# Attention in a three-mixer encoder on one core: which operand of the value product is moved, and where the rows are divided by their sums

## The chip, the cores and the metric

The kernel runs on one core of a Trainium2 chip. The metric is device time in microseconds (us). The engines that matter here are PE (TensorE: matmuls, and weight loads called PEld), DVE (VectorE), ACT (ScalarE) and POOL (GpSimd); each works through its own queue in order, and semaphores hold an instruction until what it reads is there.

## What is computed

The reference is an encoder of two layers on 512 tokens of width 1024. Each layer has three token mixers (latent attention, an mLSTM, a state-space scan called SSD), an output projection, a layer norm and 16 experts. The change touches only the end of the attention:

```python
s = (einsum('bqhd,bkhd->bhqk', qn_b, k_nope) + einsum('bqhr,bkr->bhqk', qr_b, k_rope)) * scale
p = softmax(s, axis=-1)
o = einsum('bhqk,bkhd->bqhd', p, v)      # 8 heads, v is 64 wide, 512 queries, 512 keys
```

The softmax divides each row (a query) by the sum of its exponentials. Since that sum belongs to the query and not to the key, the division may come before the product with `v` or behind it.

## The kernel before, in words

Tokens lie in four tiles of 128 (`NT = 4`). The output projection wants the attention's result with features on the partitions and tokens along the free axis: `xh[j]` and `xl[j]`, the high and low parts of 128 features (two heads, pair `j`) by 512 tokens, which `finish_heads` (line 910) writes from PSUM with one ACT copy and one DVE subtraction.

`attention()` (line 1291) gives two generators.

- `scores(hd)`, five steps for a head. The first step makes the head's queries and keys. Each of the other four takes one tile of 128 queries: three matmuls (`mm3`) into a PSUM bank of 128 queries by 512 keys, a DVE reduction for the row's maximum, an ACT exponential that writes `P` (128x512, fp32) and the row's sum, a DVE reciprocal of that sum (128x1), and then the product of `P` with it in line 1339: on POOL for heads 0 to 5, on DVE for heads 6 and 7 (`NORMV`).
- `values(hd)`, four steps for a head and two more for every second head. Each of the four takes a block `c` of 128 keys: four PE transposes turn the four `P` blocks into `PT` (keys by 512 queries), which ACT or DVE copies to SBUF. Behind the odd head comes the product for the pair. For each key block and each of the two heads, `v` is the stationary operand (128 keys by 64 features) and `PT` is moved (128 keys by 512 queries):

```python
T.matmul(po_[64 * e:64 * e + 64], vt[c][:, (2 * j + e) * 64:(2 * j + e) * 64 + 64],
         PTs[2 * j + e][c].ap, start=(c == 0), stop=(c == NT - 1), skip_group_check=True)
finish_heads(j, po_.ap)
```

The first head of the pair fills partitions 0 to 63 of the bank and the second 64 to 127, so that the bank already has the form that `finish_heads` wants. All these operands are plain fp32. A plain fp32 product stands in the trace as two MATMUL records, each with a weight load of its own (the form printed is f32 for these and for the fp32r ones alike).

`SEQ` (line 72) is a hand-written string of the order in which steps of the mixers are written: d and h the SSD, p the projections, i the attention's inputs, m the mLSTM, s `scores`, v `values`. So attention and mLSTM alternate in one stretch of each layer (about 172 to 280 us and 680 to 788 us of the profile). Within it the framework that builds the program may still move instructions of different steps past each other on an engine's queue. PSUM has eight banks; three of them (`PA`, line 251) serve the attention's keys (`pk`), queries (`pq`) and `po_`, two (`PM`) the mLSTM, three (`PT_`) the scores and the transposes. SBUF slots come from one pool of 37, and from the same pool come the buffers into which the weights of the output projection and the experts are loaded ahead.

Behind the mixers comes the output projection (line 1622 on), which takes the feature blocks in the order 6 and 7, 4 and 5, 0 and 1, and at last 2 and 3 (`order = (3, 2, 0, 1)`).

Of the kernel before, what the change touches and what calls it, by code (L numbers as in the profile page):

```python
# [13 lines left out]
AF = mybir.ActivationFunctionType  # L14
OP = mybir.AluOpType
# [5 lines left out]
NT = S // 128  # L21
# [22 lines left out]
BLK = 96  # L44
POOLP = ()
AHEAD = 1
NORMV = (6, 7)
ZP = (2, 3)
PH = 512
RK = (0, 4)  # L50
# [135 lines left out]
class Buf:  # L186
# [4 lines left out]
    def free(self):  # L191
        assert self.live
        self.live = False
        self.pool.put(self)
# [17 lines left out]
def tile_trunk(ctx: ExitStack, tc: tile.TileContext, ins, out, dbg=None, depth=DEPTH):  # L212
# [3 lines left out]
    sm = ctx.enter_context(tc.tile_pool(name="sm", bufs=2))  # L216
# [18 lines left out]
    V, A, G, T = Pinned(nc.vector, "V"), Pinned(nc.scalar, "A"), nc.gpsimd, Pinned(nc.tensor, "T")  # L235
# [3 lines left out]
    def nm(s):  # L239
        cnt[0] += 1  # L240
        return f"{s}{cnt[0]}"
# [7 lines left out]
    Q, R = View(pool, F32R), View(pool, F32)  # L249
    banks = [psp.tile([128, 512], F32, name=f"b{i}") for i in range(8)]  # L250
    PA, PB = Slots(banks[0:NPA], 512), Slots(banks[NPA:8], 512)
# [4 lines left out]
    def small(shape, dt=F32, tag="s", bufs=1):  # L256
        return sm.tile(shape, dt, name=nm(tag), tag=tag, bufs=bufs)
# [97 lines left out]
    ident = const.tile([128, 128], F32, name="ident")  # L355
# [51 lines left out]
    def split(dst_h, dst_l, src, eng=V):  # L407
        r = A.activation(dst_h, src, AF.Copy)
        eng.tensor_sub(dst_l, src, dst_h.bitcast(F32))
        return r  # L410

    def pair(src=None):

        b = Q.get()
        h, lo = b.ap[:, 0:512], b.ap[:, 512:1024]
        if src is not None:
            split(h, lo, src)
        return b, h, lo

    def mm3(p, ah, al, bh, bl, start=True, stop=True):  # L420
        T.matmul(p, ah, bh, start=start, stop=False)
        T.matmul(p, ah, bl, start=False, stop=False)
        T.matmul(p, al, bh, start=False, stop=stop)
# [134 lines left out]
    for l in range(depth):  # L558
# [351 lines left out]
        def finish_heads(j, src, scale=None):  # L910
            h, lo = xh[j], xl[j]
            if scale is None:
                split(h, lo, src)
            else:
                A.activation(h, src, AF.Identity, scale=scale)
                V.scalar_tensor_tensor(lo, src, scale, h.bitcast(F32), op0=OP.mult, op1=OP.subtract)
# [366 lines left out]
        def load_uq(g):  # L1283

            r = R.get(1024)
            load(r.ap, ins["w_uqp"], (l * 2 + g) * 128 * 1024, [[1024, 128], [1, 1024]])
            res = [pair(r[:, k * 512:(k + 1) * 512]) for k in range(2)]
            r.free()
            return res

        def attention():
            rots = mla["rots"]
            qn, kn, (ukb, ukh, ukl), vt = (mla[n] for n in ("qn", "kn", "uk", "vt"))
            uqs, Ps, PTs, pks = {}, {}, {}, {}

            def scores(hd):
                j, e = hd // 2, hd % 2
                if hd % 4 == 0:
                    uqs[hd // 4] = load_uq(hd // 4)
                uq = uqs[hd // 4]  # L1300
                if e == 0:
                    pk = pks[j] = PA.get()
                    s = slice(j * 128, (j + 1) * 128)
                    T.matmul(pk.ap, ukh[:, s], kn[1], start=True, stop=False)
                    T.matmul(pk.ap, ukh[:, s], kn[2], start=False, stop=False)
                    T.matmul(pk.ap, ukl[:, s], kn[1], start=False, stop=True)
                pk = pks[j]
                pq = PA.get()
                for k in range(2):
                    h, lo = (t[:, (hd % 4) * 128:(hd % 4 + 1) * 128] for t in uq[k][1:])  # L1310
                    T.matmul(pq.ap, h, qn[k][1], start=(k == 0), stop=False)
                    T.matmul(pq.ap, h, qn[k][2], start=False, stop=False)
                    T.matmul(pq.ap, lo, qn[k][1], start=False, stop=(k == 1))
                qf = R.get_half()
                V.tensor_mul(qf.ap, pq.ap, rots.ap)
                pq.free()
                qb, qh, ql = pair(qf.ap)
                qf.free()
                _, kh, kl = kb[e]
                A.activation(kh[0:64], pk[64 * e:64 * e + 64], AF.Copy)  # L1320
                V.tensor_sub(kl[0:64], pk[64 * e:64 * e + 64], kh[0:64].bitcast(F32))
                if e:
                    pk.free()
                if hd % 4 == 3:
                    free([b for b, _, _ in uq])
                yield
                Ps[hd] = []
                for i in range(NT):
                    s = slice(i * 128, (i + 1) * 128)
                    pS = PT_.get()  # L1330
                    mm3(pS.ap, qh[:, s], ql[:, s], kh, kl)
                    mx = small([128, 1], tag="mx", bufs=6)
                    V.tensor_reduce(mx, pS.ap, axis=AX.X, op=OP.max, negate=True)
                    P = R.get_half()
                    sums = small([128, 1], tag="sums", bufs=6)
                    A.activation(P.ap, pS.ap, AF.Exp, bias=mx, accum_out=sums)
                    pS.free()
                    V.reciprocal(sums, sums)
                    (V if hd in NORMV else G).tensor_scalar(P.ap, P.ap, sums, 0.0, op0=OP.mult, op1=OP.add)  # L1339
                    Ps[hd].append(P)  # L1340
                    if i == NT - 1:
                        qb.free()
                    yield

            def values(hd):
                j, e = hd // 2, hd % 2
                PT = PTs[hd] = []
                for c in range(NT):
                    pb = PT_.get()
                    for i in range(NT):  # L1350
                        T.transpose(pb[:, i * 128:(i + 1) * 128], Ps[hd][i][:, c * 128:(c + 1) * 128], ident)
                    t = R.get_half()
                    if hd in PTV and c % 4 == 3:
                        V.tensor_copy(t.ap, pb.ap)
                    else:
                        A.activation(t.ap, pb.ap, AF.Copy)
                    pb.free()
                    PT.append(t)
                    if c == NT - 1:
                        free(Ps[hd])  # L1360
                    yield
                if e == 0:
                    return
                po_ = PA.get()
                for c in range(NT):
                    for e in range(2):
                        T.matmul(po_[64 * e:64 * e + 64], vt[c][:, (2 * j + e) * 64:(2 * j + e) * 64 + 64],
                                 PTs[2 * j + e][c].ap, start=(c == 0), stop=(c == NT - 1), skip_group_check=True)
                    if c == 1:
                        yield  # L1370
                free(PTs[2 * j], PTs[2 * j + 1])
                finish_heads(j, po_.ap)
                po_.free()
                yield

            return chain(scores), chain(values)

        def chain(f):
            for hd in range(HEADS):
                yield from f(hd)  # L1380
# [14 lines left out]
        for n, t in enumerate(SEQ):  # L1395
            ph({"m": "mlstm", "d": "ssd", "p": "proj"}.get(t, "attn"))
            if t == "s" and "s" not in streams:
                streams["s"], streams["v"] = attention()
            next(streams[t], 1)
# [417 lines left out]
        for c in WSEQ.split():  # L1817
            if c[0] == "Z":
                i = int(c[1])
# [36 lines left out]
        for _ in range(NU):  # L1856
            m, n = todo.pop(0)
# [295 lines left out]
        for i in range(NT):  # L2153
            n = norms[i]
# [79 lines left out]
```

## Time and profile before

| what | value |
|---|---|
| median of 3 runs | 1034.4 us (1031.29 to 1034.73) |
| profiled execution's own time | 1031.19 us |
| its span, first to last instruction | 1029.5 us |
| mean granted TensorE clock | 0.989 |
| HBM read, written | 159.61 MB, 23.59 MB |

The span lies within the profiled execution's own time; 1.7 us of that lie outside it. In a row that groups instructions, the first number after the bar is the time in which at least one of the group was running, the second the mean duration of one in ns; then comes idle time of the engine ahead of them and what ended it. Matmuls overlap, so the mean of one is longer than the pace at which they follow each other. In a windows row each engine has its busy time and its count of instructions in the stretch. In a waits row stand the total, the number of waits and the longest.

### The profile page before, as it was taken

What the parts mean: (1) busy time and instruction counts of PE and PEld (TensorE: products, weight loads), DVE (VectorE), ACT (ScalarE), POOL (GpSimd) and SP (SyncE); (2) the same over time, 40 slices, a digit from 0 to 9 for tenths busy, and PEclk for the clock granted to TensorE, in tenths of its full rate; (3) what the DMA queues carried; (4) which work ended last, traced back from release to release, by engine and by line L of the source; (5) the groups of instructions that cost most, each with busy time, mean ns of one, the idle gap of its engine ahead of it and who ended that gap; (6) DMA issues with size and microseconds to landing.
All of it is one profiled execution on the core that took longest, in us unless ns stands there. A gap on an engine that the chain in (4) does not pass through costs nothing. (4 is left out here: it accounts for less than half of the span.)

```text
span 1029.5 us, 15384 instructions
## 1 busy us (share of the span) xinstructions
PE 977.3 (95%) x5326; PEld 730.0 (71%) x5326; DVE 813.6 (79%) x1808; ACT 635.4 (62%) x1176; POOL 193.0 (19%) x176
## 2 busy tenths in 40 slices
PE   6999999999998899999999999999999989999995
PEld 6976697666687666766598767875657876667663
DVE  8996566878649799999969956578795498999986
ACT  5565635566424588889645555465673246888885
POOL 1000002242003143332100000022320122333422
PEclk9999999999999899999999999999999989999998
DMA  8201200115845889999542111001349387999943
GB/s 317 72 22 63 69 3 1 42 46 181 296 174 219 274 285 340 345 329 310 170 164 72 42 42 51 1 1 41 130 161 317 130 286 260 325 339 327 323 139 161
DMA packets 51795, 176.76 MB, mean 172 GB/s; under 512 B 8170, under 2 KB 8682, under 8 KB 51713
## 3 DMA queue, kind: packets, MB, share of 16 engines
q1 hardware_dynamic: 45216, 160.42, 43.9%
q0 software_dynamic: 6496, 15.31, 6.2%
q8 instruction: 43, 0.70, 0.3%
q14 instruction: 40, 0.32, 0.1%
HBM read 159.61 MB, written 23.59 MB: 178 GB/s over the span
## 5 line engine op out<-in xcount | busy, mean ns | idle before, releaser
L229 PE MATMUL b<-xt,s 128*128 128x512 f32 (+3 forms) x1488 | 326.1, 366 | 12.7 <-ACT s L229 9.2
L229 PE MATMUL b<-s,s 128*128 128x512 f32 (+8 forms) x1308 | 321.8, 404 | 4.7 <-ACT s L229 2.9
L229 PEld LDWEIGHTS b<-xt,s 128*128 128x128 f32 (+2 forms) x1488 | 233.1, 183 | 79.5 <-issue 12.2
L229 DVE TENSOR_TENSOR s<-s,s 128x1024 fp32r<-128x1024 f32 (+8 forms) x252 | 226.3, 922 | 53.4 <-ACT s L229 46.6
L229 ACT ACTIVATE s<-s 128x1024 fp32r<-128x1024 f32 (+4 forms) x220 | 191.3, 904 | 90.5 <-PE b L229 32.4
L229 PEld LDWEIGHTS b<-s,s 128*128 128x128 f32 (+3 forms) x1308 | 182.8, 171 | 85.2 <-ACT s L229 18.6
L229 ACT ACTIVATE s<-b 128x512 f32<-128x512 f32 (+8 forms) x274 | 131.8, 499 | 174.6 <-PE b L229 169.2
L229 PE MATMUL b<-s,xt 128*128 128x256 f32 (+2 forms) x944 | 203.5, 355 | 0.4 <-DVE s L229 0.3
L229 PEld LDWEIGHTS b<-s,xt 128*128 128x128 f32 (+1 forms) x944 | 146.3, 184 | 34.7 <-issue 6.7
L229 DVE TENSOR_TENSOR xt<-s,xt 128x1024 fp32r<-128x1024 f32 (+1 forms) x107 | 127.1, 1193 | 14.0 <-ACT xt L229 13.8
L229 ACT ACTIVATE xt<-s 128x1024 fp32r<-128x1024 f32 (+1 forms) x108 | 111.6, 1043 | 26.5 <-PE b L229 18.4
L229 PE MATMUL b<-ident,s 128*128 128x128 f32 (+3 forms) x736 | 106.2, 268 | 12.3 <-DMA s<-x1d,slx 5.5
L229 PEld LDWEIGHTS b<-ident,s 128*128 128x128 f32 (+3 forms) x736 | 80.7, 150 | 44.3 <-POOL s L1339 10.4
L1599 POOL DMA_INDIRECT acc<-s,slx x28 | 58.6, 2093 | 164.1 <-ACT s L229 121.0
L229 DVE TENSOR_TENSOR s<-b,s 128x192 fp32r<-128x192 f32 (+3 forms) x108 | 57.9, 549 | 12.7 <-PE b L229 10.1
L1339 POOL TENSOR_SCALAR s<-s,sums 128x512 f32<-128x512 f32 x48 | 37.3, 780 | 150.8 <-DVE sums L229 124.9
L229 ACT ACTIVATE s<-b,mx 128x512 f32<-128x512 f32 x64 | 43.9, 692 | 18.9 <-DVE mx L229 12.6
L1447 POOL DMA_INDIRECT s<-x1d,slx x30 | 40.9, 1365 | 56.2 <-PE b L229 21.4
L229 DVE TENSOR_REDUCE mx<-b 128x1 f32<-128x512 f32 x64 | 43.5, 686 | 8.9 <-PE b L229 8.0
L229 PE MATMUL b<-xt 128*96 128x512 f32 x160 | 47.6, 404 | 1.4 <-DVE xt L229 1.4
L229 ACT ACTIVATE s<-b,slw 96x512 f32<-96x512 f32 (+1 forms) x60 | 39.1, 683 | 5.6 <-PE b L229 3.6
L229 ACT ACTIVATE s<-s,sb 128x128 f32<-128x128 f32 x64 | 25.5, 412 | 19.2 <-DVE s L229 18.8
(249 smaller groups left out, 860.8 us busy)
## 6 DMA issues: line engine op xcount, KB each, us to landing
s<-in_w_gu_dram SPq DMA_DIRECT2D x128, 512.0 KB
s<-in_expert_w_down_dram SPq DMA_DIRECT2D x64, 512.0 KB
s<-in_w_inp_dram SPq DMA_DIRECT2D x36, 512.0 KB
s<-in_w_outp_dram SPq DMA_DIRECT2D x16, 512.0 KB
x1d<-s SPq DMA_DIRECT2D x8, 512.0 KB
acc<-s SPq DMA_DIRECT2D x8, 512.0 KB
s<-acc SPq DMA_DIRECT2D x8, 512.0 KB
s<-in_x_t_dram SPq DMA_DIRECT2D x4, 512.0 KB
```

The costliest lines, as they stand in the source:

```text
L229: r = f(*a, **kw)
L1339: (V if hd in NORMV else G).tensor_scalar(P.ap, P.ap, sums, 0.0, op0=OP.mult, op1=OP.add)
L1447: self.ga = G.indirect_dma_start(out=self.xg[:BLK], out_offset=None, in_=x1d[0:128 * n, :], in_offset=bass.IndirectOffsetOnAxis(ap=ix[:BLK ...
L1599: G.indirect_dma_start(out=acc[:, :], out_offset=bass.IndirectOffsetOnAxis(ap=self.ix[:BLK, 0:1], axis=0), in_=yt[:BLK], in_offset=None, b ...
```

## The change

The row sums of a pair of heads go into one tile of 128x4x2, and the reciprocal and the product in `scores` are gone, with `NORMV`: `P` holds plain exponentials. In the value product the operands change places: each 128x128 block of `PT` is the stationary operand and the 128x64 block of `v` is moved, so that the bank holds tokens on its partitions and, along the free axis, four token tiles of two heads of 64 features. One DVE reciprocal inverts the 128x8 sums, one DVE product reads the bank and writes it, scaled, to SBUF, four PE transposes turn that into a second bank of the same three, and `finish_heads` reads it from there.

```diff
-NORMV = (6, 7)
...
+                if e == 0:
+                    sums[j] = small([128, NT, 2], tag="sums", bufs=3)
...
-                    sums = small([128, 1], tag="sums", bufs=6)
-                    A.activation(P.ap, pS.ap, AF.Exp, bias=mx, accum_out=sums)
+                    A.activation(P.ap, pS.ap, AF.Exp, bias=mx, accum_out=sums[j][:, i, e:e + 1])
                     pS.free()
-                    V.reciprocal(sums, sums)
-                    (V if hd in NORMV else G).tensor_scalar(P.ap, P.ap, sums, 0.0, op0=OP.mult, op1=OP.add)
...
                 po_ = PA.get()
                 for c in range(NT):
                     for e in range(2):
-                        T.matmul(po_[64 * e:64 * e + 64], vt[c][:, (2 * j + e) * 64:(2 * j + e) * 64 + 64],
-                                 PTs[2 * j + e][c].ap, start=(c == 0), stop=(c == NT - 1), skip_group_check=True)
+                        for i in range(NT):
+                            o = (2 * i + e) * 64
+                            T.matmul(po_[:, o:o + 64], PTs[2 * j + e][c][:, i * 128:(i + 1) * 128],
+                                     vt[c][:, (2 * j + e) * 64:(2 * j + e) * 64 + 64], start=(c == 0 and i == 0 and e == 0),
+                                     stop=(c == NT - 1), skip_group_check=True)
                     if c == 1:
                         yield
                 free(PTs[2 * j], PTs[2 * j + 1])
-                finish_heads(j, po_.ap)
+                sm = sums[j].rearrange("p i e -> p (i e)")
+                V.reciprocal(sm, sm)
+                o = R.get_half()
+                V.tensor_tensor(o.v("p (n c) -> p n c", n=2 * NT), po_.v("p (n c) -> p n c", n=2 * NT),
+                                sm[:, :, None].to_broadcast([128, 2 * NT, 64]), op=OP.mult)
                 po_.free()
+                pt_ = PA.get()
+                for i in range(NT):
+                    T.transpose(pt_[:, i * 128:(i + 1) * 128], o[:, i * 128:(i + 1) * 128], ident)
+                o.free()
+                finish_heads(j, pt_.ap)
+                pt_.free()
                 yield
```

More of the change, by code (lines that the diff above doesn't have):

```diff
@@ L1293, in attention @@
             qn, kn, (ukb, ukh, ukl), vt = (mla[n] for n in ("qn", "kn", "uk", "vt"))
-            uqs, Ps, PTs, pks = {}, {}, {}, {}
+            uqs, Ps, PTs, pks, sums = {}, {}, {}, {}, {}
             def scores(hd):
```

## The prediction

> **What bounds the kernel now.** I read the page's busy times first, then the windows of the two stretches in which the attention runs, then the waits inside them. The chain of waits on the page is no help: its shares add up to 3% of the span, the last stage alone.
>
> ```profile
> span 1029.5 us, 15384 instructions
> PE 977.3 (95%) x5326; PEld 730.0 (71%) x5326; DVE 813.6 (79%) x1808; ACT 635.4 (62%) x1176; POOL 193.0 (19%) x176
> ...
> PE 1%; DVE 1%; ACT 1%; issue 0%; DVEq 0%; ACTq 0%
> ```
>
> PE is busy nearly throughout. The windows say whether that holds where the change is made; the third and fourth are the output projection that follows in the first layer.
>
> ```profile
> 172.00:280.00 108.00, 103.06 (x532) 69.35 (x532) 82.23 (x204) 67.60 (x156) 28.76 (x35) 1.00 0.37 127
> 680.00:788.00 108.00, 104.75 (x538) 70.03 (x538) 84.12 (x207) 68.49 (x157) 29.26 (x35) 1.00 0.38 126
> ```
>
> ```profile
> 282.00:292.00 10.00, 10.00 (x58) 8.51 (x57) 6.03 (x11) 1.08 (x2) 0.00 (x0) 1.00 0.89 305
> 292.00:302.00 10.00, 9.97 (x54) 8.26 (x54) 1.72 (x4) 2.15 (x3) 0.00 (x0) 1.00 0.14 37
> ```
>
> The columns after the length are PE, PEld, DVE, ACT and POOL. In the two stretches PE is idle for 4.9 and 3.3 us of 108, together 8.2 us; no other engine comes near it (DVE 82 and 84, ACT 68, POOL 29). So what the attention adds to PE's queue is paid nearly in full, and what it takes from DVE and POOL pays only through PE's few waits. PE's waits in the first stretch, then in the second:
>
> ```profile
> PE b L229 <- POOL s L1339: 1.6, 4, 0.6
> PE b L229 <- ACT s L229: 1.5, 4, 0.7
> PE b L229 <- DVE s L229: 1.3, 2, 0.9
> ```
>
> ```profile
> PE b L229 <- ACT s L229: 1.6, 4, 0.7
> PE b L229 <- POOL s L1339: 1.1, 3, 0.5
> ```
>
> Line 1339 is the product on the probabilities. Transposes that wait for it hold PE for 1.6 + 1.1 = 2.7 us in the whole kernel.
>
> **The value product.** Per pair of heads it is 4 key blocks by 2 heads, 8 products before and 8 by 4 token tiles, 32, behind the change; with 4 pairs and 2 layers 64 against 256. Each is two records on PE, so 128 against 512. The old ones are the only matmuls with 64 stationary and 512 moved columns in these stretches:
>
> ```profile
> L229 PE MATMUL b<-s,s 128*64 128x512 f32 x62 | 19.3, 610 | 0.7 <-ACT s L229 0.7
> ```
>
> ```profile
> L229 PE MATMUL b<-s 128*64 128x512 f32 x4 | 2.1, 605 | 0.0
> ```
>
> The first row stands in both stretches with the same numbers; the second is that of the whole kernel, for records whose two operands print alike. 62 + 62 + 4 = 128, the count wanted, and they took 19.3 + 19.3 + 2.1 = 40.7 us, 0.318 each. The mean of one is 0.610, so they overlap: the two heads of a pair fill different halves of the columns and in part run side by side.
>
> The new products, 128 stationary and 64 moved columns in plain fp32, do not stand in the trace, but a near twin does. The mLSTM multiplies a 128x128 fp32 block by 65 moved columns, 64 products in 128 records:
>
> ```profile
> L229 PE MATMUL b<-s,s 128*128 128x65 f32 x128 | 15.7, 271 | 0.0
> ```
>
> ```profile
> 227.83 2.39 PE L229 MATMUL b<-s,s 128*128 128x130 f32 x20
> ```
>
> By the first row a record costs 15.7 / 128 = 0.123 us. The second is a line of the timeline with 20 such records without a gap (the first few 130 wide, most 65): less the 0.271 of the last, 19 starts in 2.12 us, 0.112 each. That 130 and 65 columns follow at the same pace says that the moved columns do not set it; the weight load does, which every record has:
>
> ```profile
> L229 PEld LDWEIGHTS b<-s,s 128*128 128x128 f32 x656 | 100.6, 190 | 32.4 <-ACT s L229 15.1 <-DVE s L229 3.0 <-issue 2.0
> ```
>
> 656 of them in 100.6 us are 0.153 each, with gaps and other forms in it; I take that as a witness that loads of this size come no denser than about a tenth of a microsecond, not as a price. Between 0.112 and 0.123 I take 0.112, since the new products come in runs of 16 products whose operands lie ready: 512 x 0.112 = 57.3 us; with 0.123 it is 63.0. So the product alone costs 57.3 - 40.7 = 16.6 us more (22.3 with the other end).
>
> A rule of the Trainium skill speaks against this change in words: TensorEngine Tiling (Array Packing), in When to Use Tiling, says that where the moved side has at most 64 columns one should swap the operands and use two column tiles, for a gain of up to two. The kernel before is that swapped form. By the full factor the products would go to 81.4 us, 40.7 more; the rows above show only part of it, since the overlap before is partial.
>
> **The transposes.** Four for each pair, 32 in all, of 128x128 fp32, like those of the probabilities.
>
> ```profile
> L229 PE MATMUL b<-ident,s 128*128 128x128 f32 x416 | 69.7, 281 | 4.9 <-POOL s L1339 2.8 <-DVE s L229 1.0 <-ACT s L229 0.5
> ```
>
> ```profile
> 208.40 1.20 PE L229 MATMUL b<-ident,s 128*128 128x128 f32 x9 [0.21 <-POOL s L1339]
> ```
>
> 69.7 / 416 = 0.168 each with their tails; in the run of nine, (1.20 - 0.28) / 8 = 0.115. 32 of them are 3.7 to 5.4 us; I take 3.7, as they come in fours.
>
> **DVE, POOL and ACT.** What goes and what the new operations are like:
>
> ```profile
> L1339 POOL TENSOR_SCALAR s<-s,sums 128x512 f32<-128x512 f32 x48 | 37.3, 780 | 150.8 <-DVE sums L229 124.9
> ```
>
> ```profile
> L229 DVE TENSOR_TENSOR s<-b,s 128x512 f32<-128x512 f32 x32 | 21.6, 684 | 10.8 <-PE b L229 10.1 <-POOL s L1132 0.5
> ...
> L229 DVE RECIPROCAL sums<-sums 128x1 f32<-128x1 f32 x64 | 9.7, 155 | 3.6 <-ACT s L229 3.2
> ...
> L229 DVE TENSOR_SCALAR s<-s,sums 128x512 f32<-128x512 f32 x16 | 8.8, 558 | 0.1
> ...
> L229 DVE RECIPROCAL dn<-dn 128x8 f32<-128x8 f32 x8 | 1.5, 193 | 0.0
> ```
>
> POOL loses 37.3 us, all beside other work. DVE loses 9.7 + 8.8 = 18.5 and gains 8 x (0.193 + 0.684) = 7.0, so it gets 11.5 us lighter. PE waits on DVE for 1.3 us in the first stretch and not in the second; I count 1 us of it as gone. ACT keeps its exponentials, the readings of their sums and the copies. The 2.7 us that PE waited for line 1339 go; what is late next is the exponential itself, on ACT, from which these transposes then hang. ACT has room (68 of 108), but the earlier product also gave the queue time, so I count all 2.7 only because PE has more other work to do meanwhile.
>
> **The new wait.** In each pair the four transposes wait for the DVE product, that one for the last of the 32 matmuls, and behind the transposes PE's queue holds the next scores, mLSTM products and transposes. `finish_heads` waits in turn, one reciprocal, one product and four transposes later than before. If the framework puts them right behind the products, PE stands for 0.193 (if the reciprocal comes late), 0.684, and the rest of whatever DVE is doing; if other matmuls stand between, nothing. No such wait is in the trace of before, so I bound it by 0 and by two DVE operations of 0.684 and the reciprocal, 1.6 us, eight times: 0 to 12.5 us. The nearest row is PE's wait on DVE, 2 times and 1.3 us among all the DVE results that matmuls read in the first stretch, so I take a value near zero: 2 us in all. At the end of the stretch the wait has cover: the last pair is features 2 and 3 or earlier, the output projection takes these last, and the windows to 302 us show PE full. Should the cover be gone, it costs 1.6 us in each layer. The second bank comes from the same three (`PA`), with one more turn in each pair; a bank late by a DVE product is within the same bound.
>
> **The sum.** 16.6 + 3.7 - 2.7 - 1 + 2 = 18.6 us, against 1031.2 of the profiled execution: 1049.8. The median of the runs stands 3.2 us above that execution (1034.4), so the median should be 1053. Smallest: the low prices, all 8.2 us of PE's idle time gone, no new wait: 16.6 + 3.7 - 8.2 = 12.1, which is 1043.3 in the profile and 1046.5 as a median. Largest without the full new wait: 22.3 + 5.4 - 2.7 = 25.0, 1056.2 or 1059.4.
>
> **The rivals.**
>
> One: the moved columns set the pace after all, and the kernel gets faster. The old record costs 0.318 us for 512 columns, so one for 64 would cost 0.040, and 512 of them 20.4 us: 40.7 - 20.4 = 20.3 us less, with 3.7 for the transposes and 3.7 of waits gone, 1031.2 - 20.3 = 1010.9. It decides from the point where weight loads hide fully behind other matmuls, below 0.079 us a record (40.7 / 512). The skill's page TensorE: Matmul & The Clock Gate, Back-to-back issue gap, would even put 64 columns at about 60 cycles, 25 ns, which would make 12.8 us of the 512. Against it stand the 65-wide records at 0.112 and above, of the same kind and in the same queue. 3%.
>
> Two: PE is less full than it looks, since the ends of matmuls are modelled and a matmul that follows late looks joined. Then the added 20.3 us fill hidden gaps and the time stays within 3 us, 1028 to 1034 in the profile. For it: 10.4 us of weight loads waited on line 1339, of which only 2.7 show as PE idle.
>
> ```profile
> PEld b L229 <- POOL s L1339: 10.4, 18, 1.0
> ```
>
> Against it: all of that is 10.4, half of what is added, and the other waits of the loads, on ACT, stay. 4%.
>
> Three: the new wait is met in full, 12.5 us instead of 2: 1060.3 in the profile, 1063.5 as a median. For it: the transposes stand right behind the products in the program. Against: the framework already lets other steps' matmuls stand between a head's steps. It decides where fewer than about six scores matmuls are ready in the queue behind the products. 13%.
>
> Four: DMA sets the pace of the experts, and a later attention is made up there. The window to 302 us has a DMA share of 0.14: the loads ahead have run out of slots, so they start again only when the stages behind move, and everything moves with them. I give it no chance of its own.
>
> **How the numbers follow.** The forecast has 80%, rival one 3%, two 4%, three 13%. A measurement of this kernel tells from no change about 0.3%, 3 us. Faster 0.03, same 0.03 (most of rival two), slower 0.94. The range runs from 1043, the smallest sum with half of the spread of the runs (1.6 us, and 2 for what the order on PE's queue may bring), to 1064, rival three as a median.
>
> **What would show it.** In the profile of the changed kernel: 512 records of form 128*128 128x64 at 0.110 to 0.125 us each, 55 to 63 us; none of 128*64 128x512 in these stretches; 32 more transposes; no line 1339 on POOL; both stretches about 9 us longer, PE over 95% busy in them, the rest of the kernel as long as before. It would be wrong if the records came at under 0.09 or over 0.15 us, if PE's waits on DVE rose by over 5 us, or if the stretches grew by under 5 us each.

## The result and the profile after

| | before | changed |
|---|---|---|
| median of 4 runs each, us | 1034.57 (1031.29 to 1035.49) | 1048.88 (1043.56 to 1057.44) |
| profiled execution, us | 1031.19 | 1047.73 |

The ratio is 1.0138, with a 95% interval of 1.0101 to 1.0176: 14.3 us slower by the medians, where 18.6 were forecast.

The page of the changed kernel answers to the two lines quoted first in the prediction:

```profile
span 1046.0 us, 16076 instructions
PE 994.1 (95%) x5742; PEld 782.9 (75%) x5742; DVE 805.9 (77%) x1744; ACT 635.5 (61%) x1176; POOL 153.4 (15%) x128
```

PE is 16.8 us busier and the span 16.5 longer; PE's share stays at 95%. To see where it went, the span is cut at two marks in each layer, the first exponential of the attention and the first matmul of the router, that lie on both sides of the changed stretch. The windows between them, first of the kernel before, then of the changed one (length; then busy times of PE, PEld, DVE, ACT, POOL):

```profile
173.70:289.60 115.90, 110.96 (x570) 75.83 (x568) 88.00 (x210) 68.25 (x156) 28.76 (x35) 1.00 0.42 142
682.50:796.60 114.10, 110.85 (x569) 75.15 (x567) 87.92 (x208) 67.91 (x156) 29.26 (x35) 1.00 0.43 143
```

```profile
175.00:298.10 123.10, 118.81 (x779) 101.85 (x777) 84.34 (x178) 68.67 (x156) 10.74 (x11) 1.00 0.40 134
691.20:812.20 121.00, 117.95 (x777) 101.32 (x775) 83.56 (x176) 67.68 (x156) 10.46 (x11) 1.00 0.42 136
```

The stretches grew from 230.0 to 244.1 us, 7.2 and 6.9, and everything else by 2.4. PE's busy time in them grew by 14.9 us (221.8 to 236.8) and its idle time hardly moved (8.2 to 7.3). POOL lost 37 us and DVE 8; what that is worth by itself is asked in the first experiment. PE's waits in the two stretches of the changed kernel:

```profile
PE b L228 <- DVE s L228: 3.1, 4, 0.9
PE b L228 <- ACT s L228: 1.2, 2, 0.7
```

```profile
PE b L228 <- ACT s L228: 2.4, 2, 2.0
PE b L228 <- DVE s L228: 0.6, 1, 0.6
```

The 2.7 us for line 1339 are gone, the waits for ACT went from 3.1 to 3.6 us and those for DVE from 1.3 to 3.7. Of the latter, one wait is for the late product, ahead of the four transposes of one pair:

```profile
207.12 0.66 PE L228 MATMUL b<-ident,s 128*128 128x128 f32 x4 [0.73 <-DVE s L228]
```

The signs named in the prediction mostly came: 512 records, none of the old form in these stretches, 32 more transposes, no line 1339, PE over 95% busy in them. The stretches grew by 7 us each instead of 9, and PE's waits on DVE rose by 2.4 us, under the 5 that would have counted against it.

The matmuls of the changed kernel by form:

```profile
L228 PE MATMUL b<-ident,s 128*128 128x128 f32 x448 | 69.5, 279 | 4.0 <-ACT s L228 2.0 <-DVE s L228 1.7
...
L228 PE MATMUL b<-s,s 128*128 128x64 f32 x480 | 57.9, 271 | 0.0
...
L228 PE MATMUL b<-s 128*128 128x64 f32 x32 | 4.2, 275 | 0.0
```

480 + 32 = 512 records took 57.9 + 4.2 = 62.1 us, 0.121 each; the transposes rose from 416 to 448 and took no more in all (69.7 before). One view shows something that the prediction had not looked at: what the weight loads waited for in the first stretch, before and after.

```profile
PEld b L229 <- ACT s L229: 12.3, 21, 1.0
PEld b L229 <- issue: 8.8, 26, 0.8
PEld b L229 <- POOL s L1339: 5.3, 9, 0.9
```

```profile
PEld b L228 <- ACT s L228: 5.9, 16, 1.0
PEld b L228 <- DVE s L228: 5.8, 10, 1.2
PEld b L228 <- issue: 0.4, 1, 0.4
```

"issue" is waiting for nothing that another engine does. It falls from 8.8 us to 0.4 with the old product's form; in the two stretches of the kernel before, 49 of the 51 such waits stand at loads next to or within that form.

### The profile page after: what moved, and what is told of

Same layout as the page of the kernel before. It is cut to its first block, busy times and chain, and to the rows that moved or that the text cites. A ratio compares the mean times of both kernels' runs of the same rounds, so it can differ in the third digit from the quotient of the medians.

```text
span 1046.0 us, 16076 instructions
## 1 busy us (share of the span) xinstructions
PE 994.1 (95%) x5742; PEld 782.9 (75%) x5742; DVE 805.9 (77%) x1744; ACT 635.5 (61%) x1176; POOL 153.4 (15%) x128
## 5 line engine op out<-in xcount | busy, mean ns | idle before, releaser
L228 PE MATMUL b<-s,s 128*128 128x64 f32 (+9 forms) x1664 | 334.9, 349 | 4.8 <-DVE s L228 2.9
L228 PEld LDWEIGHTS b<-s,s 128*128 128x128 f32 (+3 forms) x1664 | 230.4, 180 | 67.2 <-DVE s L228 13.8
L228 ACT ACTIVATE xt<-s 128x1024 fp32r<-128x1024 f32 (+1 forms) x108 | 111.6, 1043 | 26.9 <-PE b L228 18.7
L228 PE MATMUL b<-ident,s 128*128 128x128 f32 (+2 forms) x768 | 104.9, 267 | 11.3 <-DMA s<-x1d,slx 5.2
L228 PEld LDWEIGHTS b<-ident,s 128*128 128x128 f32 (+2 forms) x768 | 83.8, 151 | 28.9 <-DVE s L228 6.7
L1611 POOL DMA_INDIRECT acc<-s,slx x28 | 56.1, 2003 | 165.0 <-ACT s L228 132.8
L1459 POOL DMA_INDIRECT s<-x1d,slx x30 | 40.7, 1358 | 58.2 <-PE b L228 23.8
L228 ACT ACTIVATE xt<-b 128x384 fp32r<-128x384 f32 (+1 forms) x56 | 26.9, 528 | 23.6 <-PE b L228 23.5
```

The costliest lines, as they stand in the source:

```text
L228: r = f(*a, **kw)
L1459: self.ga = G.indirect_dma_start(out=self.xg[:BLK], out_offset=None, in_=x1d[0:128 * n, :], in_offset=bass.IndirectOffsetOnAxis(ap=ix[:BLK ...
L1611: G.indirect_dma_start(out=acc[:, :], out_offset=bass.IndirectOffsetOnAxis(ap=self.ix[:BLK, 0:1], axis=0), in_=yt[:BLK], in_offset=None, b ...
```

## The experiments

The theory was that the turned product is the price, that its weight loads set its pace, and that the rest is small. The rivals: the late division and what waits for it; the moved columns; a PE with hidden room. All ratios are against the kernel before, run beside it on the same chip; the stretches are the two of above, from one profiled execution of each kernel, with 230.0 us for the kernel before. They leave out what varies outside them, where all fourteen kernels do the same work and took 797.8 to 805.7 us. The granted clock was full in the stretches except where it is said.

**The division left out.** From the kernel before:

```diff
-                    V.reciprocal(sums, sums)
-                    (V if hd in NORMV else G).tensor_scalar(P.ap, P.ap, sums, 0.0, op0=OP.mult, op1=OP.add)
```

> The kernel before without the reciprocals and without the product on the probabilities (line 1339), nothing put in their place: the division by the rows' sums is left out. It measures alone what the change takes away. Theory (the price is the turned value product, paced by its weight loads; the rest is small): PE's 2.7 us of waits for line 1339 go and about 1 us on DVE, so 3 to 4 us less than before, about 1031. Rival (the division held far more than the waits show, and its going hides part of a dearer product): 8 us or more less, 1026 or below.

Measured: 1031.16 us against 1033.52, ratio 0.9970 (0.9952 to 0.9988), stretches 226.0. The division was worth 3 to 4 us, the size that its waits say, but not by their way. The windows:

```profile
177.60:291.30 113.70, 109.85 (x571) 76.22 (x569) 81.31 (x170) 67.89 (x156) 11.04 (x11) 1.00 0.42 145
685.20:797.50 112.30, 109.08 (x569) 75.88 (x567) 81.05 (x168) 67.20 (x156) 10.46 (x11) 1.00 0.42 146
```

PE's idle time fell by 1.1 us only (8.2 to 7.1): the 2.7 us for line 1339 went, and the waits for ACT rose from 3.1 to 6.1. The other 2.9 us are PE's busy time (221.8 to 218.9), though its matmuls are the same, so some waiting is counted there as busy. These 3 to 4 us are about what leaving out the early division can win on the kernel before.

**The turned product with the early division.** From the changed kernel, with the two lines above back in `scores`:

```diff
-                V.tensor_tensor(o.v("p (n c) -> p n c", n=2 * NT), po_.v("p (n c) -> p n c", n=2 * NT),
-                                sm[:, :, None].to_broadcast([128, 2 * NT, 64]), op=OP.mult)
+                V.tensor_copy(o.ap, po_.ap)
```

> The kernel behind the change, but with the probabilities divided as before, on POOL and DVE, and a plain DVE copy in place of the late division; the turned product and the transposes back stay. It computes all. Theory: all of the price is here and the gain of the early division's going is not: 3 to 5 us above the changed kernel (1048.9), about 1053, so 18 above before. Rival (the price is the late division and what waits for it): the copy costs the queue as much as the late product did, but with the sums long done; 1040 or less.

Measured: 1057.44 us against 1033.52, ratio 1.0229 (1.0205 to 1.0252), stretches 252.7. The price is with the turned product and its transposes. The clock was at half for 3.4 us of the first stretch; counting 1.7 us of that as lost (an estimate, by the last section), 251.0 is left. So the gain of dividing late is larger here than on the old product, about 7 us of the stretches against 4.0, where 3 to 5 were expected. PE stands idle for 10.8 us in them, against 7.3 in the changed kernel.

**No late chain.** From the changed kernel, `finish_heads(j, po_.ap)` right behind the products; the late division and the four transposes are gone.

> The kernel behind the change without the late division and without the four transposes back for each pair: the bank of the turned product goes straight to the high and low parts, with tokens where features should be. The division and the transposition are left out. Theory: the 32 transposes (3.7 us) and at most 2 us of waits go, so 4 to 6 us below the changed kernel, 1043 to 1045, still about 10 above before. Rival (the late chain is the price): it falls to 1036 or below.

Measured: 1040.55 us, ratio 1.0061 (1.0039 to 1.0083), stretches 235.4. Between the kernel without division and this one stands the turned product alone, 226.0 to 235.4 or 9.4 us; between this one and the changed kernel the late chain, 8.7 us. So the theory holds for little more than half of the price, and the late chain costs more than forecast; the time lies below the 1043 to 1045 that were expected. The windows of this kernel:

```profile
173.10:292.40 119.30, 116.24 (x762) 100.70 (x760) 80.77 (x170) 68.00 (x156) 11.09 (x11) 1.00 0.40 138
688.90:805.00 116.10, 114.89 (x760) 99.98 (x758) 80.07 (x168) 67.74 (x156) 10.62 (x11) 1.00 0.42 142
```

PE is idle for 4.3 us here and for 7.1 in the kernel without division (226.0 less 109.85 and 109.08 busy): the added matmuls filled 2.8 us of waits.

**Twice the moved columns.** From the changed kernel:

```diff
-                            o = (2 * i + e) * 64
-                            T.matmul(po_[:, o:o + 64], PTs[2 * j + e][c][:, i * 128:(i + 1) * 128],
-                                     vt[c][:, (2 * j + e) * 64:(2 * j + e) * 64 + 64], ...
+                            o = i * 128
+                            T.matmul(po_[:, o:o + 128], PTs[2 * j + e][c][:, i * 128:(i + 1) * 128],
+                                     vt[c][:, 2 * j * 64:2 * j * 64 + 128], ...
```

> The kernel behind the change with 128 moved columns in each of the turned products instead of 64 (the values of both heads of the pair, so that the two heads' sums mix: the result is another one), the same stationary blocks and the same number of records. Theory (the weight loads set the pace, 0.112 us a record): the time of the changed kernel, 1048.9, within 3 us. Rival (the moved columns set the pace): 512 records with 64 columns more, at 0.053 us for 64 of 128 columns side by side with the 0.112, 27 us more, 1076.

Measured: 1045.25 us, ratio 1.0112 (1.0089 to 1.0136), stretches 245.7; the changed kernel had 1.0138 and 244.1. The clock was at half for 3.4 us of the first stretch; without the 1.7 us of that (the same estimate) it is 244.0. Twice the columns cost nothing that can be measured, so the moved columns do not set the pace. A row of the changed kernel's trace goes down to a single moved column:

```profile
L228 PE MATMUL b<-ones,s 128*128 128x1 f32 x80 | 9.3, 244 | 0.0
```

That is 0.116 us a record. What all these records share is a weight load of 128 columns, and in the changed kernel's trace such loads of two slots follow each other at 0.112 us in the median. So the load is the likely pace; no run changed the load alone, and another fixed cost of a record is not excluded.

**Each turned product twice.**

```diff
                         for i in range(NT):
                             o = (2 * i + e) * 64
-                            T.matmul(...)
+                            for n in range(2):
+                                T.matmul(...)
```

> The changed kernel with each of the turned products issued twice into the same sums (so that they come out doubled: the result is another one). 512 records more. Theory (PE is full in these stretches, and a record costs its weight load): 512 x 0.109 = 56 us more, 1102 to 1106. Rival (PE has hidden room): under 45 us more, below 1094.

Measured: 1103.24 us, ratio 1.0700 (1.0641 to 1.0759), stretches 300.9, 56.8 more than in the changed kernel for 512 records: 0.111 each, or 0.104 when the 3.4 us that 6.8 us at half clock cost in the first stretch are taken off (an estimate). PE's idle time fell from 7.3 to 5.5 us: little of what was added found room.

**The old product at full width.** From the kernel before, 128 stationary columns into the whole bank:

```diff
-                        T.matmul(po_[64 * e:64 * e + 64], vt[c][:, (2 * j + e) * 64:(2 * j + e) * 64 + 64],
-                                 PTs[2 * j + e][c].ap, start=(c == 0), stop=(c == NT - 1), skip_group_check=True)
+                        T.matmul(po_.ap, vt[c][:, 2 * j * 64:2 * j * 64 + 128],
+                                 PTs[2 * j + e][c].ap, start=(c == 0 and e == 0), stop=(c == NT - 1), skip_group_check=True)
```

> The kernel before with 128 stationary columns in each value product (the values of both heads of the pair) instead of 64, into all 128 partitions of the bank: the same number of records and moved columns, no half-width form and nothing side by side. The two heads' sums mix, the result is another one. Theory: 128 records at 0.422 us are 54 us against 39, less 30 entries and 30 exits of the half-width form at about 0.1 us: about 10 to 13 us above before, 1045, near the changed kernel. Rival (changing the form costs what the overlap gains): within 3 us of before.

Measured: 1049.88 us against 1034.63, ratio 1.0149 (1.0124 to 1.0173), stretches 245.7. Two heads in half-width form (64 stationary columns each), in part side by side, are worth 15 us, a little more than the 10 to 13 expected.

**The old products grouped.** From the kernel before, each product of a pair also waits for the copy of the pair's last block:

```diff
+                        if c < 3:
+                            tc.add_manual_dep(r.ins, PTs[2 * j + 1][3].cp.ins.name, ...)
```

> The kernel before, complete, with one thing more: the eight value products of a pair wait for the copy of the pair's last block of probabilities, so that they stand together on PE's queue and the two heads' products lie side by side. In the trace of before, the 128 records take 39 us from start to start, and each of some 30 entries into the half-width form takes another 0.093 us; together, at 0.422 us for two side by side, they would take 8 x (8 x 0.422 + 0.2) = 28.6 us. Theory (what the old product costs is set by how much the heads overlap): 10 to 13 us less than before, about 1023. Rival (PE's waits take it back, since the products start later): within 3 us of before.

Measured: 1034.88 us against 1034.63, ratio 0.9997 (0.9978 to 1.0015). The theory fell here, and the time is what the rival said. The windows:

```profile
175.60:290.90 115.30, 108.36 (x571) 76.98 (x569) 89.44 (x210) 68.00 (x156) 27.79 (x35) 0.99 0.40 138
683.80:798.40 114.60, 107.97 (x569) 75.73 (x567) 87.48 (x207) 67.99 (x156) 27.70 (x35) 0.99 0.40 138
```

PE is 5.5 us less busy than before (216.3 against 221.8) and 5.4 us more idle (13.6 against 8.2). Work taken from PE came back as waits, above all for ACT, 7.8 us where the kernel before had 3.1 (first stretch, then second):

```profile
PE b L229 <- ACT s L229: 3.4, 6, 1.0
```

```profile
PE b L229 <- ACT s L229: 4.4, 6, 1.4
```

One wait, 0.85 us on DVE, is that of a grouped product itself; the others are of other steps' matmuls, which the products no longer stand between. But waits are not all. Each stretch has a piece in which the granted clock was at half, and those of the kernel before have none:

```profile
244.60:248.00 3.40, 3.40 (x9) 2.62 (x10) 2.49 (x8) 2.00 (x4) 0.70 (x1) 0.51 0.47 171
708.80:712.30 3.50, 3.50 (x11) 1.22 (x9) 3.10 (x10) 1.78 (x4) 2.06 (x3) 0.51 0.15 19
```

By the count of the last section they cost 3.4 us together, so that at full clock the stretches would take about 226.5 us, 3.5 less than before (an estimate). It is not this execution alone: the mean granted clock was 0.982 over the twelve of this kernel and 0.986 over the sixteen beside it, which by that count is 4 us. So at equal clock the shorter product would have gained some 4 us, by the same estimate. In the 3.4 us ahead of each piece PE was busy for 2.04 and 1.52 us only, so its waits may be what lowered the clock; no run here tests that.

**The late chain, taken apart.** Five kernels asked why it costs 8.7 us and not the 5.7 of the forecast. First the transposes and `finish_heads` of a pair moved behind the second block of transposes of the next pair (a list `late` holds them; the last pair stays):

```diff
+                    if c == 1 and late:
+                        late.pop()()
```

> The changed kernel, complete, with the four transposes back and the making of the high and low parts of a pair moved behind the second block of transposes of the next pair (the last pair stays). Theory (of the 8 us that the late chain costs, half is waiting for the DVE product and what it pushes aside): 3 to 5 us below the changed kernel, 1044 to 1046. Rival (it is the work of the transposes itself, or the order elsewhere): within 2 us of the changed kernel.

Measured: 1049.06 us, ratio 1.0135 (1.0104 to 1.0166), stretches 244.4: no difference. Then the late product kept, but unread, with `finish_heads(j, po_.ap)` behind it:

> The changed kernel with its late reciprocal and its late DVE product still there, but with nothing reading what that product writes: no transposes back, and the bank of the turned product goes straight to the high and low parts. The division's effect and the transposition are left out. It splits the 8 us between the changed kernel and the one without the late chain. Theory (DVE has room, and the price is the four transposes): within 2 us of the kernel without the late chain, 1.004 to 1.008 of before. Rival (DVE is short in some places of the stretch, and the late product pushes the row maxima): 3 us or more above it, 1.009 or more of before.

Measured: 1036.14 us against 1034.83, ratio 1.0025 (1.0005 to 1.0044), stretches 235.3. So the late DVE work costs nothing in the stretches (235.4 without it). The ratio is even lower than without it, which the clock can explain: 0.987 in the mean here, 0.982 there. It also says how far the split can be trusted. With this kernel in the middle, the ratios give 5.7 us for the turned product (0.9970 to 1.0025) and 11.7 for the transposes back (1.0025 to 1.0138), where the stretches give 9.3 and 8.8. Then the transposes back, reading a block that lies ready:

```diff
-                    T.transpose(pt_[:, i * 128:(i + 1) * 128], o[:, i * 128:(i + 1) * 128], ident)
+                    T.transpose(pt_[:, i * 128:(i + 1) * 128], PTs[2 * j + 1][0][:, i * 128:(i + 1) * 128], ident)
```

> The changed kernel with its late product still there, but with the four transposes of each pair reading a block of probabilities that lies ready instead of that product, so that they need not wait for it; the result is another one. Theory (the transposes cost their work on PE and what follows them, not a wait): within 2 us of the changed kernel, 1.012 to 1.016 of before. Rival (waiting for the late product): 3 us or more below it, 1.011 or less.

Measured: 1051.83 us, ratio 1.0162 (1.0141 to 1.0183), stretches 249.1. Without the wait for the late product it is no faster, rather slower. This kernel also gives the slots of the pair's `PT` back later, behind the transposes, which may be why it is slower. With the single wait of 0.73 us in the changed kernel's trace and the delayed chain above, which gained nothing, it says that the wait which the prediction priced is not what costs. What came with the transposes besides their work is a second PSUM bank in each pair, and a copy on ACT that stands in its queue until they are made. Two kernels parted these:

```diff
-                pt_ = PA.get()
+                pt_ = PT_.get()
```

> The changed kernel, complete, with the bank of the four transposes back taken from the three that serve the scores and the transposes of the probabilities instead of the three that serve keys, queries and the value product. Theory one (the second bank in each pair makes keys, queries and the next value product late): 3 to 5 us below the changed kernel, 1.009 to 1.011 of before. Theory two (ACT stands at the copy of the high part until PE has made the transposes, 15 us in the two stretches against 6 before, and what is behind it comes late): within 2 us of the changed kernel, 1.012 to 1.016.

Measured: 1043.47 us against 1034.08, ratio 1.0114 (1.0079 to 1.0148), stretches 240.4, 3.7 below the changed kernel's; the ratio lies just above what theory one expected.

```diff
-                finish_heads(j, pt_.ap)
+                V.tensor_copy(xh[j], pt_.ap)
+                V.tensor_sub(xl[j], pt_.ap, xh[j].bitcast(F32))
```

> The changed kernel, complete, with the high part of each attention pair copied by DVE instead of ACT, so that ACT does not stand in its queue waiting for the transposes back. DVE gets 8 copies of 0.69 us more. Theory two (ACT's standing there is what the late chain costs beside the work of the transposes): 3 to 5 us below the changed kernel, 1.009 to 1.011 of before. Theory one (the banks): no gain, 1.012 to 1.018, since the same wait then stands on DVE.

Measured: 1047.59 us, ratio 1.0137 (1.0115 to 1.0159), stretches 243.9: no difference. ACT's standing falls as a cause. For the banks, the windows of the kernel with the bank moved:

```profile
176.80:298.30 121.50, 118.44 (x779) 101.60 (x777) 85.92 (x178) 67.90 (x156) 10.41 (x11) 1.00 0.40 135
690.80:809.70 118.90, 117.80 (x777) 101.45 (x775) 84.63 (x176) 67.67 (x156) 10.43 (x11) 1.00 0.42 138
```

PE works 236.2 us, as in the changed kernel (236.8), and is idle for 4.2 instead of 7.3. That speaks for the bank, but the intervals of the two ratios overlap, and the order on the queues changed with it. The one long wait in the changed kernel, 2.0 us in the second stretch, is of a transpose of probabilities for its exponential; with the bank moved it is 0.6 us, as in the two kernels without the transposes back. The bank stays likely, not shown.

## Why the prediction was right, point by point

**What bounds the stretch.** Right: PE's work is paid nearly in full, and what DVE and POOL lose is not (50 us less busy without the division, for 4.0 us). It is sharper when work is added than when it is taken off. Adding 512 records to the full PE cost 56.8 us. Grouping the old products, which took 5.5 us of busy time from PE, gained nothing in the time: PE waited 5.4 us longer, and its clock was lower.

**The price of a record.** Right: 0.108 to 0.121 us, with 64 moved columns or 128, as the 65-wide twin said. The times from each record of PE to the start of the next, idle time included, summed by form over the two stretches (us, with the count of records), give the product's own price:

```
                                before      no division   no late chain       changed
turned product                                             55.2 (512)      55.7 (512)
old product, half width      39.0 (128)    39.4 (128)
128x128 transposes           35.6 (288)    36.2 (288)      29.5 (288)      35.9 (320)
128x512, both from slots     72.9 (256)    69.1 (256)      69.4 (256)      70.3 (256)
128x512, slots and xt        49.0 (194)    47.0 (194)      48.2 (194)      48.2 (194)
all                         229.0         224.9           234.4           243.0
```

55.2 - 39.4 = 15.8 us, where 16.6 were forecast.

**The step that missed in size: "So the product alone costs 57.3 - 40.7 = 16.6 us more".** Alone it cost 9.4 by the stretches. The subtraction took the neighbours as they were, and the old product had made them dearer. A transpose followed by a half-width product took 0.203 us in the median to the next start, against 0.109 before another transpose; a 128x512 product 0.326 against 0.234. The 29 entries into the form in the stretches of the kernel before make some 2.7 us, and with the turned product the form never changes there. The weight loads' waits on "issue" go with it. TensorEngine Tiling (Array Packing) of the Trainium skill, Key Properties, says that a change of the tiling mode drains the engine; the trace fits that, with 0.09 us on the way in and 0.10 on the way out (0.522 instead of 0.422 for the last half-width record). Another 2.8 us went into waits that the longer product filled. That makes 15.8 - 2.7 - 2.8 = 10.3; the last microsecond is not assigned.

**The transposes and the new wait.** Forecast 3.7 + 2, measured 8.7. This term was too small. The work is near the forecast: PE is 4.5 us busier with the transposes than with the late product unread (236.8 against 232.3). The rest is 4.3 us of PE's idle time (7.3 against 3.0), and mostly not for the reason given: the transposes hold PE for the late product once, for 0.73 us, and the idle time is no shorter when they need not wait. Moving the second bank to other banks took 3.1 us of it away in the trace. The prediction had put that bank "within the same bound"; it is likely the larger part.

**The waits that go.** Forecast 2.7 + 1, measured 4.0 on the old product, of which idle time was 1.1. The size came out by some luck: the waits for line 1339 were replaced by others, and what shrank was PE's busy time. With the turned product it was about 7, so these terms do not add up independently. Why is open: line 1339 holds PE for 1.4 us there, less than the 2.7 before.

**The sum.** 9.4 + 8.7 - 4.0 = 14.1 us in the stretches, where 16.6 + 5.7 - 3.7 = 18.6 stood. Two errors, of 7 and 3 us, cancelled in part, which was luck; the sign was right, and so was the price of a turned record. Which of the two parts is the larger is not settled, since the ratios put the late chain ahead (11.7 against 5.7); by both measures the product alone is under its forecast and the late chain over it.

**The rivals.** The moved columns as the pace (rival one) are excluded by the kernel with 128 of them. The Trainium skill's page TensorE: Matmul & The Clock Gate, Back-to-back issue gap, gives about 25 ns for up to 64 columns as the gap of a matmul by itself, and says that weight loads and matmuls set the spacing together in a stream of both. The second holds here: 0.109 us, where every product brings a new 128-column weight block in fp32. Hidden room (rival two) is true in small: some waiting counts as busy (2.9 us, by the kernel without division), but nearly all of the added work was paid. The full wait on the late product (rival three) did not happen. The later attention was not made up behind it (rival four): outside the stretches the changed kernel took 801.9 us, the kernel before 799.5. The factor of up to two for column tiles (the Trainium skill, TensorEngine Tiling (Array Packing), Theoretical Speedup) was 1.35 here: 52.5 us of starts with the old product at full width, 39.0 with the column tiles.

## What to carry to other kernels

Price a small matmul by its records, not by its moved columns: with 128 stationary and 64 or 128 moved columns a plain fp32 record cost the same tenth of a microsecond here. Making the wide operand stationary multiplied the records by four, at a third of the old price each. When a form of matmul is taken out, look at what stood beside it too. And on an engine that is 96% busy with waits close behind, added work costs its price less the waits it fills, while work taken off may gain little; take terms one by one on the chip before adding them. Look at the granted clock of a stretch before comparing its length.

## What the runs showed of the hardware

The four executions of the changed kernel differ by 14 us, and the mean granted TensorE clock goes with it: spans of 1041.8, 1046.0, 1048.3 and 1055.7 us at 0.989, 0.986, 0.986 and 0.975. Counting the span times one less the clock as lost, 11.5, 14.6, 14.7 and 26.4 us, leaves 1030.3, 1031.4, 1033.6 and 1029.3: a spread of 14 us becomes one of 4. In the profiled executions the recorded clock is full, except that it is at half for pieces of 3.4 us or a few of them in a row, and for the last 9 to 12 us of the span. The same count is the estimate used above for a stretch with such a piece. It is a rough one: outside the stretches, where all fourteen profiled executions do the same, it narrows 797.8 to 805.7 us only to 783.8 to 790.3. Of the 16.5 us between the profiled executions of before and changed, 2.4 lie outside the changed stretches, and there the clock lost 3.9 us more in the changed one. So a profiled execution is compared by stretches, and by their clock, rather than by its span.
